# Diagonal and first-level products of the gated recurrence issued in one step

## The chip, the cores and the metric

The kernel runs on one core of one Trainium2 chip. The metric is the device time of one execution in microseconds, as a median of several runs. The engines are TensorE (PE, with its weight loads PEld), VectorE (DVE), ScalarE (ACT), GpSimd (POOL) and SyncE (SP), which issues nearly all DMAs. A matmul writes to PSUM, which has eight banks; the others read from there.

## The reference

One layer of a hybrid decoder for 1024 prompt tokens and 64 sample tokens: a gated feed-forward, then a mixer of sliding-window attention and a gated linear recurrence side by side, then a second gated feed-forward. Only the recurrence is touched by the change. For each of four heads (keys and values 128 wide), with a forget gate f and k = 1 - f, it computes in chunks

```python
def step(S, inp):
    qb, kb, gb, vb = inp                      # gb = log f
    G = jnp.cumsum(gb, axis=2)
    diff = G[:, :, :, None, :] - G[:, :, None, :, :]
    decay = jnp.exp(jnp.where(causal, diff, -jnp.inf))
    A = jnp.einsum('bhtk,bhsk,bhtsk->bhts', qb, kb, decay)
    o = jnp.einsum('bhts,bhsv->bhtv', A, vb) + jnp.einsum('bhtk,bhkv->bhtv', qb * jnp.exp(G), S)
    G_last = G[:, :, -1:, :]
    S = jnp.exp(G_last[:, :, 0, :])[..., None] * S + jnp.einsum(
        'bhsk,bhsv->bhkv', kb * jnp.exp(G_last - G), vb)
    return S, o
```

The entry A[t, s] is the product of q at t and k at s, with every key channel damped by the gates of the positions after s up to t. All is in float32.

## The kernel before

The 1088 tokens are cut into three groups: group 0 has 256 prompt tokens and the 64 sample tokens, groups 1 and 2 have 384 prompt tokens each. Most of the time goes into dense projections; each product of two float32 operands is made of three matmuls over high and low parts (`mm3`, L283 to L285), with the parts formed by a cast on ACT (L260) and a subtraction on DVE or POOL (L261). They write to four PSUM banks with the tag `mm`; everything else shares the other four, tag `ax` (`axbank`).

The recurrence works in blocks of 128 tokens (two in group 0, three in each of groups 1 and 2) and one block of the 64 sample tokens. `intra` (L1256 on) forms the matrix A of a block, transposed, in `At`. It avoids exponentials of sums by a tree: at level h (1, 2, 4 ... 64, for samples up to 4) it pairs neighbouring runs of h tokens, queries from the right run, keys from the left. First Q = q f on DVE (L1264), K = 1 - f on ACT (L1265), `At` is cleared on POOL (L1267), and the products of f over runs of 2, 4, ... tokens are formed on POOL (L1284). The function `blocks` issues one burst of matmuls into one `ax` bank: for four heads, and for each run of 32 tokens, a 32 x 32 product (L1276), 16 matmuls a block, which the trace shows as 32 records. It is called once for the diagonal (`ld`, from K and the unchanged q), whose result DVE multiplies by a 32 x 32 identity into `C` (L1288), and then for each level up to 16 (`lv`, from K and Q), whose result DVE copies into `C` where the level's mask allows (L1295). After each level DVE multiplies the right runs of Q (L1311), and POOL the left runs of K (L1313), by the products of f. Levels 32 and 64 have products of their own (L1300) that ACT copies to `At` (L1303). `hgrn_block` then applies `At` and the carried state to the values, and updates the state; `sample_hgrn` does that for the samples; `finish_hgrn` normalises and gates the output.

All these are Python generators: each `yield` ends a step. The projections of the mixer and the feed-forward products around it call `tick` after each half of a projection (each such call is a unit), and `pace` then lets the two queues of mixer work, attention (`at`) and recurrence (`hg`), take as many steps as they owe:

```python
for k, q in queues.items():
    sofar, rate = 0, 0.0
    for n, _, left in q:
        sofar += left
        rate = max(rate, sofar / max(1, DUE[n] - now[0]))
    owed[k] += rate
```

`left` is the number of steps that a generator still has, given by hand in `ready` (12 for a block, 18 for the sample block), and `DUE` the unit by which group n is to be through (132, 208, 256). Counted in the code, the recurrence of the groups 0, 1 and 2 is handed over at units 36, 128 and 188. What is left over at units 136, 216 and 268 would be run off at once by `need_mix`. A scheduler plans the instructions of each engine from these, by priority and by a simulated time, so that the order on an engine need not be that of the code.

Of the kernel before, what the change touches and what calls it, by code (L numbers as in the profile page):

```python
# [27 lines left out]
NPB = [2, 3, 3]  # L28
# [15 lines left out]
def tile_step(ctx: ExitStack, tc: tile.TileContext, A: dict, O: list):  # L44
# [10 lines left out]
    def uid(s):  # L55
        cnt[0] += 1
        return f"{s}_{cnt[0]}"
# [4 lines left out]
    def axbank(s="ax"):  # L62
        return ps.tile([P, 512], F32, tag="ax", bufs=4, name=uid(s))
# [243 lines left out]
    def new_h(n):  # L307
        return [[hslot(n), hslot(n)], [hslot(n), hslot(n)]]
# [739 lines left out]
    def mixing(tp, h):  # L1048
# [5 lines left out]
        def m2(shape=(P, 512)):  # L1054
            return tp.tile(list(shape), F32, tag="m2", bufs=6, name=uid("m2"))
# [34 lines left out]
        def col_tile(c):  # L1090
# [3 lines left out]
            return load_up(w_in, c * P)  # L1094

        def w_in_units(n, ready):
            w = WIDTH[n]
            npb = NPB[n]
# [157 lines left out]
        def intra(n, c0, r, top, last_q, res):  # L1256

            z = Z[n]
            f, q = [z[i][:, :, c0:c0 + r] for i in ("f", "hq")]
            Q, K, D = m2((P, 4, P)), m2((P, 4, P)), m2()
            V.tensor_tensor(Q[:, :, :r], q, f, op=ALU.mult)  # L1264
            S.activation(K[:, :, :r], f, AF.Copy, bias=1.0, scale=-1.0)  # L1265
            At = tp.tile([P, 4, P], F32, tag="At", bufs=1, name=uid("At"))
            G.memset(At, 0.0)  # L1267
            C = tp.tile([P, 4, 32], F32, tag="cm", bufs=2, name=uid("cm"))
            nq = r // 32

            def blocks(s, x, y):
                b4 = axbank(s).rearrange("p (a t) -> p a t", a=4)
                for a in range(4):
                    for i in range(nq):
                        cs = slice(32 * i, 32 * i + 32)
                        PE.matmul(b4[cs, a, :32], x[:, a, cs], y[:, a, cs], start=True, stop=True)  # L1276
                return b4

            Ds, off, h = [f], 0, 1
            while h <= top:  # L1280
                nx = r // (2 * h)
                Dv = Ds[-1].rearrange("p a (x e) -> p a x e", e=2)
                Ds.append(D[:, off:off + 4 * nx].rearrange("p (a x) -> p a x", a=4))
                G.tensor_tensor(Ds[-1], Dv[:, :, :, 0], Dv[:, :, :, 1], op=ALU.mult)  # L1284
                off += 4 * nx
                h *= 2
            b4 = blocks("ld", K, q)
            V.tensor_tensor(C[:r], b4[:r, :, :32], ident32[:r].unsqueeze(1).to_broadcast([r, 4, 32]),  # L1288
                            op=ALU.mult)
            yield  # L1290
            h = 1
            while h <= top:
                if h <= 16:
                    b4 = blocks("lv", K, Q)
                    V.copy_predicated(C[:r], lmask[h][:r].unsqueeze(1).to_broadcast([r, 4, 32]), b4[:r, :, :32])  # L1295
                else:
                    b4 = axbank(f"l{h}").rearrange("p (a t) -> p a t", a=4)
                    for c in range(0, r, 2 * h):
                        for a in range(4):
                            PE.matmul(b4[c:c + h, a, :h], K[:, a, c:c + h], Q[:, a, c + h:c + 2 * h],  # L1300
                                      start=True, stop=True)
                    for c in range(0, r, 2 * h):
                        S.copy(At[c:c + h, :, c + h:c + 2 * h], b4[c:c + h, :, :h])  # L1303
                if h == min(top, 16):
                    for i in range(nq):
                        G.tensor_copy(At[32 * i:32 * i + 32, :, 32 * i:32 * i + 32], C[32 * i:32 * i + 32])
                nx = r // (2 * h)
                Qv, Kv = [t[:, :, :r].rearrange("p a (x u) -> p a x u", u=2 * h) for t in (Q, K)]
                Dv = Ds.pop(0).rearrange("p a (x e) -> p a x e", e=2)
                if last_q or h < top:  # L1310
                    V.tensor_tensor(Qv[:, :, :, h:], Qv[:, :, :, h:], Dv[:, :, :, 0:1].to_broadcast([P, 4, nx, h]),  # L1311
                                    op=ALU.mult)
                G.tensor_tensor(Kv[:, :, :, :h], Kv[:, :, :, :h], Dv[:, :, :, 1:2].to_broadcast([P, 4, nx, h]),  # L1313
                                op=ALU.mult)
                h *= 2
                yield
            res += [At, Q, K, Ds[0]]

        def finish_hgrn(n, bank, r, c0):
            sm = small()  # L1320
            o = m2((P, 4, P))
            b4 = bank.rearrange("p (a t) -> p a t", a=4)
            for a in range(4):
                S.activation(o[:r, a], b4[:r, a], AF.Square, accum_out=sm[:r, 0, a:a + 1])
            V.tensor_scalar(sm[:r, 0, :4], sm[:r, 0, :4], 1.0 / P, EPS, op0=ALU.mult, op1=ALU.add)
            root(sm[:r, 1, :4], sm[:r, 0, :4])
            V.tensor_tensor(o[:r], b4[:r], sm[:r, 1, :4].unsqueeze(2).to_broadcast([r, 4, P]), op=ALU.mult)
            yield
            tb = axbank("hT").rearrange("p (a t) -> p a t", a=4)
            for a in range(4):  # L1330
                PE.transpose(tb[:, a, :r], o[:r, a], ident[:r, :r])
            m = m2((P, 4, P))
            V.tensor_tensor(m[:, :, :r], tb[:, :, :r], Z[n]["g"][:, :, c0:c0 + r], op=ALU.mult)
            put_mix(n, 1, slice(c0, c0 + r), m[:, :, :r])
            yield

        def hgrn_block(n, b):
            z = Z[n]
            c0 = b * P
            first = state[0] is None  # L1340
            if first:
                state[0] = tp.tile([P, 4, P], F32, tag="st", name="st")
            st = state[0]
            res = []
            yield from intra(n, c0, P, 64, not first, res)
            At, Q, K, D = res
            tb = axbank("kT").rearrange("p (a t) -> p a t", a=4)
            for a in range(4):
                PE.transpose(tb[:, a], K[:, a], ident)
            kn = m2((P, 4, P))  # L1350
            V.tensor_copy(kn, tb)
            yield
            ob = axbank("av")
            for a in range(4):
                PE.matmul(ob[:, a * P:(a + 1) * P], At[:, a], z["v"][:, b, a * P:(a + 1) * P],
                          start=True, stop=first)
                if not first:
                    PE.matmul(ob[:, a * P:(a + 1) * P], Q[:, a], st[:, a], start=False, stop=True)
            yield
            ub = axbank("u").rearrange("p (a t) -> p a t", a=4)  # L1360
            for a in range(4):
                PE.matmul(ub[:, a], kn[:, a], z["v"][:, b, a * P:(a + 1) * P], start=True, stop=True)
            if first:
                V.tensor_copy(st, ub)
            else:
                for a in range(4):
                    V.scalar_tensor_tensor(st[:, a], st[:, a], D[:, a], ub[:, a],
                                           op0=ALU.mult, op1=ALU.add)
            yield from finish_hgrn(n, ob, P, c0)
# [80 lines left out]
        def sample_hgrn():  # L1450
            n, c0, r = 0, 256, NS
            z = Z[n]
            res = []
            yield from intra(n, c0, r, 4, True, res)
            At, Q, K, D = res
            tb = axbank("skT").rearrange("p (a t) -> p a t", a=4)
# [51 lines left out]
        def ready(kind, n):  # L1508
            if n not in MT:
                MT[n] = new_h(n)  # L1510
            if kind == "at":
                gens = [(attn_block(n, b), 9) for b in range(NPB[n])]
                if n == 0:
                    gens += [(sample_attn(), 17), (kv_out(0), 1)]
                if n == 2:
                    gens.append((kv_out(2), 1))
            else:
                gens = [(hgrn_block(n, b), 12) for b in range(NPB[n])]
                if n == 0:
                    gens.append((sample_hgrn(), 18))  # L1520
                if n == 2:
                    gens.append((state_out(), 1))
            queues[kind] += [[n, g, left] for g, left in gens]

        def state_out():
            nc.sync.dma_start(O[4][0, 0].rearrange("h k v -> k h v"), state[0])
            yield
# [55 lines left out]
    h = {}  # L1583
# [195 lines left out]
```

## Time and profile before

| what | us |
|---|---|
| median of three runs | 1987.83 |
| lowest and highest of them | 1987.05, 1988.56 |
| the profiled execution, its own time | 1987.58 |
| its span | 1985.9 |
| mean granted TensorE clock | 0.998 |
| first diagonal product starts | 721.2 |
| last diagonal product starts | 1264.3 |

The profile is of one execution. Its span goes from the first instruction to the last; the time of the execution is 1.7 us longer. The lines of the profile that matter are shown with the prediction, each with what it says.

### The profile page before, as it was taken

What the parts mean: (1) busy time and instruction counts of PE and PEld (TensorE: products, weight loads), DVE (VectorE), ACT (ScalarE), POOL (GpSimd) and SP (SyncE); (2) the same over time, 40 slices, a digit from 0 to 9 for tenths busy, and PEclk for the clock granted to TensorE, in tenths of its full rate; (3) what the DMA queues carried; (4) which work ended last, traced back from release to release, by engine and by line L of the source; (5) the groups of instructions that cost most, each with busy time, mean ns of one, the idle gap of its engine ahead of it and who ended that gap; (6) DMA issues with size and microseconds to landing.
All of it is one profiled execution on the core that took longest, in us unless ns stands there. A gap on an engine that the chain in (4) does not pass through costs nothing.

```text
span 1985.9 us, 34410 instructions
## 1 busy us (share of the span) xinstructions
PE 1969.5 (99%) x13309; PEld 1849.6 (93%) x13309; DVE 1363.3 (69%) x2008; ACT 942.2 (47%) x1672; POOL 593.0 (30%) x559
## 2 busy tenths in 40 slices
PE   9999999999999999999999999999999999999998
PEld 8999999999998987798899898999999999999887
DVE  5876656886557656875566665755988888655666
ACT  6643333444445445644444555655544444444453
POOL 0014323655113101321223423301166565510202
PEclk9999999999999999999999999999999999999999
DMA  8554344656677645765444343556466555577874
GB/s 251 161 154 142 132 173 157 205 185 221 224 242 217 182 134 164 221 194 153 123 107 146 97 124 104 166 161 203 153 196 210 194 194 182 211 232 236 287 261 142
DMA packets 372988, 359.53 MB, mean 181 GB/s; under 512 B 41598, under 2 KB 295369, under 8 KB 372809
## 3 DMA queue, kind: packets, MB, share of 16 engines
q1 hardware_dynamic: 370969, 355.37, 56.8%
q8 instruction: 104, 1.70, 0.4%
q10 hardware_dynamic: 1856, 1.97, 0.3%
q14 instruction: 59, 0.48, 0.1%
HBM read 279.33 MB, written 78.94 MB: 180 GB/s over the span
## 4 chain that ended last, share of the span: by engine, by line
PE 93%; DMA 3%; DVE 2%; ACT 1%; issue 1%; POOL 0%; SPq 0%; DVEq 0%; POOLq 0%; ACTq 0%
PE mm L283 28%; PE mm L285 27%; PE mm L284 27%; PE c L285 1%; PE c L283 1%; PE c L284 1%; PE pv L1240 1%; DMA xt<-in_x_prompt_dram 1%; PE sc L1201 1%; PE lv L1276 1%; PE pT L1227 1%; PE tr L503 1%; DMA ar<-fa 1%; DMA raw<-in_ffn_w_gu_dram 1%; DVE w L261 0%
## 5 line engine op out<-in xcount | busy, mean ns | idle before, releaser
L283 PE MATMUL mm<-h,wsph 128*128 128x320 f32 (+1 forms) x1296 | 416.4, 322 | 0.7 <-ACT wsph L611 0.7
L285 PE MATMUL mm<-h,wspl 128*128 128x320 f32 (+1 forms) x1296 | 410.9, 318 | 1.7 <-DVE wspl L261 1.5
L284 PE MATMUL mm<-h,wsph 128*128 128x320 f32 (+1 forms) x1296 | 410.8, 317 | 0.0
L260 ACT CAST wsph<-raw 128x1024 fp32r<-128x1024 f32 x200 | 209.0, 1047 | 302.2 <-PE mm L284 224.3
L261 DVE TENSOR_TENSOR wspl<-raw,wsph 128x1024 fp32r<-128x1024 f32 x200 | 249.8, 1251 | 143.6 <-ACT wsph L260 142.8
L261 DVE TENSOR_TENSOR w<-raw,w 128x512 fp32r<-128x512 f32 (+1 forms) x226 | 241.6, 1073 | 79.5 <-ACT w L260 77.8
L260 ACT CAST w<-raw 128x512 fp32r<-128x512 f32 (+1 forms) x226 | 169.5, 754 | 244.1 <-PE mm L284 113.8
L283 PEld LDWEIGHTS mm<-h,wsph 128*128 128x128 f32 x1296 | 244.0, 188 | 6.1 <-issue 3.0
L285 PEld LDWEIGHTS mm<-h,wspl 128*128 128x128 f32 x1296 | 243.8, 188 | 3.8 <-DVE wspl L261 1.8
L284 PEld LDWEIGHTS mm<-h,wsph 128*128 128x128 f32 x1296 | 244.2, 188 | 1.9 <-issue 1.4
L283 PE MATMUL mm<-h,w 128*128 128x384 f32 x704 | 235.8, 335 | 0.3 <-DVE big L804 0.3
L284 PE MATMUL mm<-h,w 128*128 128x384 f32 x704 | 235.8, 335 | 0.0
L285 PE MATMUL mm<-h,w 128*128 128x384 f32 x704 | 230.5, 335 | 0.0
L788 POOL TENSOR_TENSOR big<-big 128x384 f32<-128x384 f32 x88 | 113.4, 1288 | 271.4 <-ACT big L801 161.0
L283 PE MATMUL mm<-w,h 128*128 128x512 f32 x462 | 181.8, 396 | 1.8 <-DVE big L984 1.0
L284 PE MATMUL mm<-w,h 128*128 128x512 f32 x462 | 180.5, 391 | 0.0
L285 PE MATMUL mm<-w,h 128*128 128x512 f32 x462 | 179.9, 393 | 0.0
L261 DVE TENSOR_TENSOR w<-t,w 128x512 fp32r<-128x512 f32 x176 | 163.0, 939 | 13.1 <-ACT w L260 13.1
L254 POOL TENSOR_TENSOR sm<-sm,mhalf 128x3 f32<-128x3 f32 (+4 forms) x37 | 35.2, 953 | 394.4 <-DVE sm L338 96.6
L283 PEld LDWEIGHTS mm<-h,w 128*128 128x128 f32 x704 | 132.2, 188 | 0.6 <-DVE big L804 0.6
L284 PEld LDWEIGHTS mm<-h,w 128*128 128x128 f32 x704 | 132.2, 188 | 0.0
L285 PEld LDWEIGHTS mm<-h,w 128*128 128x128 f32 x704 | 131.7, 188 | 0.0
(358 smaller groups left out, 4034.0 us busy)
## 6 DMA issues: line engine op xcount, KB each, us to landing
raw<-in_ffn_w_gu_dram SPq DMA_DIRECT2D x154, 512.0 KB
raw<-in_ffn_w_down_dram SPq DMA_DIRECT2D x74, 512.0 KB
raw<-in_w_in_dram SPq DMA_DIRECT2D x54, 512.0 KB
ar<-fa SPq DMA_DIRECT2D x70, 384.0 KB
big<-in_ffn_w_down_dram SPq DMA_DIRECT2D x88, 256.0 KB
fb<-big SPq DMA_DIRECT2D x44, 512.0 KB
raw<-fb SPq DMA_DIRECT2D x40, 512.0 KB
fa<-big SPq DMA_DIRECT2D x22, 768.0 KB
```

Source lines behind the costliest of these rows:

```text
L254: G.tensor_tensor(y, x, mhalf[:y.shape[0], :y.shape[1]], op=ALU.pow)
L260: S.copy(hi, src)
L261: (lo_eng or V).tensor_tensor(lo, src, hi.bitcast(F32), op=ALU.subtract)
L283: PE.matmul(out, a[0], b[0], start=first, stop=False, skip_group_check=resume)
L284: PE.matmul(out, a[0], b[1], start=False, stop=False, skip_group_check=resume)
L285: return PE.matmul(out, a[1], b[0], start=False, stop=last, skip_group_check=resume)
L503: PE.transpose(bank[:, i * P:(i + 1) * P], y[kh][:, i, k * P:(k + 1) * P], ident)
L788: G.tensor_tensor(e[:, i], e[:, i], e[:, i + 1], op=ALU.mult)
L1201: PE.matmul(banks[g][:, i * 256:i * 256 + wk], zq[64 * g:64 * g + 64, 2 * pr + i, b * P:(b + 1) * P], kx[64 * g:64 * g + 64, k0:k0 + wk], ...
L1227: PE.transpose(bank[:, (i * nk + kb) * P:(i * nk + kb + 1) * P], pt[g][:, i, kb * P:(kb + 1) * P], ident)
L1240: PE.matmul(ob[:, c:c + 64], pT[g][:, (i * nk + kb) * P:(i * nk + kb + 1) * P], vn[:, vb, g * 64:g * 64 + 64], start=kb == 0, stop=kb == n ...
L1276: PE.matmul(b4[cs, a, :32], x[:, a, cs], y[:, a, cs], start=True, stop=True)
```

## The change

The diagonal product and the product of level 1 are issued one after the other, ahead of the masking of the diagonal, and the `yield` between the two is gone. Level 1 then takes the bank that was already filled. The number of steps given to the pacing falls from 12 to 11 for a block and from 18 to 17 for the sample block.

```diff
@@ -1285,13 +1285,13 @@
                 off += 4 * nx
                 h *= 2
             b4 = blocks("ld", K, q)
+            b1 = blocks("lv", K, Q)
             V.tensor_tensor(C[:r], b4[:r, :, :32], ident32[:r].unsqueeze(1).to_broadcast([r, 4, 32]),
                             op=ALU.mult)
-            yield
             h = 1
             while h <= top:
                 if h <= 16:
-                    b4 = blocks("lv", K, Q)
+                    b4 = b1 if h == 1 else blocks("lv", K, Q)
                     V.copy_predicated(C[:r], lmask[h][:r].unsqueeze(1).to_broadcast([r, 4, 32]), b4[:r, :, :32])
                 else:
                     b4 = axbank(f"l{h}").rearrange("p (a t) -> p a t", a=4)
@@ -1515,9 +1515,9 @@
                 if n == 2:
                     gens.append((kv_out(2), 1))
             else:
-                gens = [(hgrn_block(n, b), 12) for b in range(NPB[n])]
+                gens = [(hgrn_block(n, b), 11) for b in range(NPB[n])]
                 if n == 0:
-                    gens.append((sample_hgrn(), 18))
+                    gens.append((sample_hgrn(), 17))
                 if n == 2:
                     gens.append((state_out(), 1))
             queues[kind] += [[n, g, left] for g, left in gens]
```

## The prediction

> **What bounds the kernel now.** I read the page first, for the engine that sets the end, then the chain that ended last, then the stretches of 50 us in which that engine is not full, then the instructions around the products that the change moves.
>
> ```profile
> span 1985.9 us, 34410 instructions
> PE 1969.5 (99%) x13309; PEld 1849.6 (93%) x13309; DVE 1363.3 (69%) x2008; ACT 942.2 (47%) x1672; POOL 593.0 (30%) x559
> ...
> PE 93%; DMA 3%; DVE 2%; ACT 1%; issue 1%; POOL 0%; SPq 0%; DVEq 0%; POOLq 0%; ACTq 0%
> ```
>
> TensorE (PE) is busy for 1969.5 of 1985.9 us, and 93% of the chain lies on it. So an edit can gain in two ways only: by making PE's own work denser, or by closing one of the few gaps, 16.4 us in all. The stretches show where the gaps are (columns: PE busy with its instructions, PEld, DVE, ACT, POOL, granted clock, DMA share, GB/s):
>
> ```profile
> 750.00:800.00 50.00, 48.99 (x323) 39.11 (x322) 35.14 (x66) 29.57 (x62) 10.48 (x18) 1.00 0.53 163
> 800.00:850.00 50.00, 47.92 (x388) 39.63 (x387) 38.90 (x62) 27.83 (x59) 16.11 (x17) 1.00 0.73 220
> ...
> 1100.00:1150.00 50.00, 50.00 (x501) 45.59 (x500) 32.44 (x64) 24.43 (x41) 17.54 (x24) 1.00 0.37 110
> ```
>
> The recurrence runs from the first diagonal product at 721 us to about 1300 us. In that time only the first two of these stretches lose much, 1.01 and 2.08 us, together 3.1 us; DVE is at 70 and 78% there. The third stands for the later blocks: PE without a gap, DVE at 65%. The other gaps lie before, after, or in the tail, where the change has no instruction.
>
> **The change, part by part.** In each of nine blocks (eight of the prompt, one of the samples) the diagonal product `ld`, the first-level product `lv`, and the masking of `ld` move into one step; one `yield` goes. No instruction is added or removed, and no DMA is issued in the steps that move, so SP's queue is passed by nothing but what the shifted pacing brings. What can change is where the product bursts stand on PE, when DVE reads them, and how the steps are spread.
>
> *The bursts.* First an `ld` that stands alone in a stream of projections, then one with `lv` right behind it (start, duration, engine, line, operation):
>
> ```profile
> 963.87 0.34 PE L284 MATMUL mm<-h,wsph 128*128 128x384 f32 x1
> 964.04 0.34 PE L285 MATMUL mm<-h,wspl 128*128 128x384 f32 x1
> 964.31 0.46 PE L1276 MATMUL ld<-big,m 128*32 128x32 f32 x32
> 964.70 0.44 PE L283 MATMUL mm<-h,wsph 128*128 128x384 f32 x1
> 964.98 0.34 PE L284 MATMUL mm<-h,wsph 128*128 128x384 f32 x1
> ```
>
> ```profile
> 1110.56 0.34 PE L284 MATMUL mm<-h,wsph 128*128 128x384 f32 x1
> 1110.83 0.46 PE L1276 MATMUL ld<-big,m 128*32 128x32 f32 x32
> 1111.10 0.49 PE L1276 MATMUL lv<-m,m 128*32 128x32 f32 x32
> 1111.52 0.44 PE L285 MATMUL mm<-h,wspl 128*128 128x384 f32 x1
> 1111.80 0.34 PE L283 MATMUL mm<-h,wsph 128*128 128x384 f32 x1
> ```
>
> In the stream one projection starts 0.17 us after another (963.87 to 964.04). From the last one before the lone burst to the second one behind it takes 964.98 - 964.04 = 0.94 us, where two intervals would be 0.34: a lone burst costs 0.60 us. The same stretch around the pair is 1111.80 - 1110.56 = 1.24 us: the second burst adds 0.30 us. So each pair that stands apart now and together later saves 0.60 - 0.30 = **0.30 us**.
>
> The saving is there because going in and out of a burst costs time: `ld` is 0.39 us from the next start when a projection follows, 0.27 us when `lv` follows. Whether a burst of another shape beside it saves as much is seen where output transposes stand between the two, and where they stand alone:
>
> ```profile
> 1162.14 0.46 PE L1276 MATMUL ld<-big,m 128*32 128x32 f32 x32
> 1162.53 0.66 PE L1180 MATMUL oT<-ident,t 128*128 128x128 f32 x4
> 1163.12 0.46 PE L1276 MATMUL lv<-m,m 128*32 128x32 f32 x32
> 1163.51 0.41 PE L285 MATMUL mm<-h,wspl 128*128 128x320 f32 x1
> ```
>
> ```profile
> 1215.42 0.60 PE L1180 MATMUL oT<-ident,t 128*128 128x128 f32 x4
> 1215.78 0.48 PE L283 MATMUL mm<-wsph,h 128*128 128x512 f32 x1
> ```
>
> `ld` to the transposes is 0.39 us, as to a projection, and the transposes take 0.59 us to the next start with `lv` behind them against 0.36 us with a projection behind. Only the same shape saves. Ordered `ld`, `lv`, transposes, this place takes 0.27 + 0.42 + 0.36 = 1.05 us instead of 0.39 + 0.59 + 0.39 = 1.37, again some 0.3 us. The Trainium skill, TensorEngine Tiling (Array Packing), section Key Properties, says that a change of the tiling mode drains TensorE; the trace agrees, with 0.39 us out of the burst against 0.27 us within it. By that rule alone, a neighbour of another shape would save nothing, which is also what these rows say.
>
> *How many pairs stand apart.* The windows open at each `ld`, 0.6 us long, PE records of L1276 only (the sample block has 16 a burst, the others 32):
>
> ```profile
> 721.20:721.80 0.60, 0.46 (x32) 1.00 0.00 0
> 788.60:789.20 0.60, 0.46 (x32) 1.00 1.12 360
> 867.00:867.60 0.60, 0.45 (x16) 1.00 1.13 342
> 964.30:964.90 0.60, 0.46 (x32) 1.00 0.06 17
> 1035.70:1036.30 0.60, 0.46 (x32) 1.00 0.64 167
> 1110.80:1111.40 0.60, 0.57 (x64) 1.00 1.15 347
> 1162.10:1162.70 0.60, 0.46 (x32) 1.00 0.43 89
> 1210.40:1211.00 0.60, 0.50 (x58) 1.00 0.07 27
> 1264.00:1264.60 0.60, 0.54 (x62) 1.00 0.00 0
> ```
>
> Three blocks already hold about 64 records: the scheduler has put `lv` right behind `ld`, although half a projection lies between them in the code. Nothing is to be had there. Five prompt blocks show 32: 5 x 0.30 = 1.5 us. The sample block has half the records; nothing (if it stays apart) and 0.30 us bound it, I take 0.2. Sum: **-1.7 us**. The bounds of this term are 0, if no pair moves, and 9 x 0.30 = 2.7 us, if all nine counted.
>
> *DVE.* The masking and the predicated copy now become ready together. What they wait for today, and how long a bank is held, shows the block with the fullest DVE:
>
> ```profile
> 782.90 0.68 DVE L1264 TENSOR_TENSOR m<-big,big 128x512 f32<-128x512 f32 x1
> ...
> 793.18 0.28 DVE L1288 TENSOR_TENSOR cm<-ld,ident 128x128 f32<-128x128 f32 x1
> ...
> 798.08 0.29 DVE L1295 COPY_PREDICATED cm<-lm,lv 128x128 f32<-128x128 uint8 x1
> 798.27 0.44 DVE L1311 TENSOR_TENSOR m<-m,big 128x256 f32<-128x256 f32 x1
> ```
>
> Q (L1264) is ready 5 us before its `ld` at 788.6, so `lv` behind `ld` has its operand; the cover is that Q and K are formed when their buffers come free, not in the step. If that cover were gone, `lv` would wait for 0.68 us of DVE. `ld` is read only 4.5 us after it was issued. With both products issued together two of the four `ax` banks are held over that lag. That costs nothing while PE needs no third and fourth bank in it, and up to the DVE work brought forward, 0.29 (L1295) + 0.44 (L1311) = 0.73 us a block, if PE waits for what DVE does next. Bounds: 0 and 9 x 0.73 = 6.6 us. Below nothing I see no reason here, since DVE does the same work. I take 0, as PE does not wait in the block that holds both banks now, at 1111 us: the stretch from 1100 to 1150 us has no gap.
>
> *The pacing.* A group's steps are spread evenly from the unit in which they are handed over to the unit in which they are due. The first group has 2 x 12 + 18 = 42 steps in units 36 to 132, then 2 x 11 + 17 = 39: one step in 2.46 units instead of 2.29. A block's share of the way is 12/42 = 0.286 before and 11/39 = 0.282 after; in the second group it is a third both times. So blocks begin and end where they did, by a unit or two, and the last step is still due at 132, 208 and 256; what follows (output transposes, the projection behind them) is not moved. Inside a block there is more time between levels. What it could free is one row, in which PE waits 1.25 us for a level's operand:
>
> ```profile
> 824.93 0.56 PE L1300 MATMUL l<-m,m 128*32 128x32 f32 x16 [1.25 <-DVE m L1311]
> ```
>
> It is the only such wait, and it lies in the gaps counted above. Which steps fall beside attention steps changes too; as only bursts of one shape save by standing together, I give that nothing, with half a microsecond to either side as an estimate (two pairs of 0.30).
>
> **Sum.** -1.7 us (bursts) + 0 (DVE) + 0 (pacing) = -1.7 us, 0.09%. Against the profiled execution's own span that is 1985.9 - 1.7 = 1984.2 us; its own time was 1987.58 us, 0.25 below the median 1987.83 of the runs shown, so the span and the median differ by a fixed amount and the median goes to **1986.1 us**. A measurement of this kernel can tell about 0.2% from no change, 4.0 us: faster means below 1983.9, slower above 1991.8.
>
> **Rivals.**
>
> 1. *The change doesn't do what it says:* the order on PE is the scheduler's, not the code's. For it: it moved `lv` over half a projection in three blocks. Against it: with nothing between the two in the code and both operands ready 5 us early, it has no ready work of earlier rank to put between. Time: 1987.8. A page bears on a near relative: bursts bound by issue, so that nothing is saved by joining them. Rows speak against that, 0.30 us for the second burst instead of 0.60. The Trainium skill, TensorEngine Tiling (Array Packing), section Instruction Overhead, gives each matmul about 60 cycles whatever its size; the trace does not show that as the limit here. Both together 0.15.
>
> 2. *More is gained:* the wider spacing also closes the gaps of the stretch from 750 to 850 us, 3.1 us. For it: DVE is fullest there and the one wait for a level lies there. Against it: most of that loss has other causes, as the chain's 3% of DMA says, and the change takes no DVE or DMA work away. Time: 1987.8 - 1.7 - 3.1 = 1983.0. Chance 0.10.
>
> 3. *Slower, DVE before evictions:* the joined masking, predicated copy and Q product stand on DVE ahead of the additions that free projection banks, and PE waits. Price 0.73 us a block; 9 x 0.73 - 1.7 = +4.9, time 1992.7. It decides from (4.0 + 1.7)/9 = 0.63 us of wait per block on. For it: the lag of 4.5 us at 788 us. Against it: only two of the 50 us stretches are short of PE work, so two or three blocks pay rather than nine, and those only 1.5 to 2.2 us. Chance 0.13 for slower by over 0.2%.
>
> 4. *A reshuffle in the gapped stretch* without a net direction: the order of evictions, weight splits and loads is planned anew, and the 3.1 us there become up to 6: -1.7 + 3.1 = +1.4, time 1989.2. Chance 0.17.
>
> **How the numbers follow.** The forecast, 1984.8 to 1987.3, has 0.45; with rivals 1 (0.15) and 4 (0.17) that is no measurable change, 0.77, of which I move 0.03 to the two sides. Faster 0.12, same 0.74, slower 0.14. The range goes from a little under rival 2 to just under rival 3: 1982.5 to 1991.5, leaving some 2 in 10 out.
>
> **What would show it.** Right: the nine windows at `ld` all hold about 64 records (32 for the sample block), a stretch of 1.24 us around each, as many instructions as before, PE's gaps outside the tail still about 3 us between 750 and 850 us. Wrong in the first term: records other than L1276 between `ld` and `lv`. Wrong in the DVE term: a wait of PE for L1288 or L1295, or longer waits of L283 for L984, in the list of waits. Wrong in the pacing: PE gaps in the stretch from 1100 to 1150 us, where there are none now. The prediction fails as a whole if the time moves by over 4 us with all pairs joined; then the cause is the order of other work, not the bursts.

## The result: 14 us slower, lost at two places

| kernel | median, us | lowest to highest | profiled span |
|---|---|---|---|
| before | 1988.03 | 1985.99 to 1988.56 | 1985.9 |
| after | 2001.99 | 2000.71 to 2004.07 | 1999.0 |

The ratio is 1.0077, with a 95% interval from 1.0067 to 1.0086. The first lines of the page of the changed kernel:

```profile
span 1999.0 us, 34396 instructions
PE 1974.6 (99%) x13309; PEld 1852.2 (93%) x13309; DVE 1361.2 (68%) x2008; ACT 943.3 (47%) x1672; POOL 594.0 (30%) x559
```

The page hardly changes: PE is busy 99% again, and its 13309 instructions are the same. Of the 13.1 us between the two spans, 8.0 are idle time of PE (1999.0 - 1974.6 = 24.4 against 16.4) and 5.1 are PE being busy for longer (1974.6 against 1969.5). Where the idle time lies is seen in stretches of 50 us of the changed kernel (columns as in the prediction):

```profile
750.00:800.00 50.00, 49.23 (x355) 39.82 (x354) 35.69 (x68) 28.80 (x62) 8.15 (x14) 1.00 0.52 161
800.00:850.00 50.00, 45.40 (x339) 37.44 (x338) 36.88 (x58) 27.60 (x58) 16.22 (x17) 0.93 0.70 210
850.00:900.00 50.00, 47.87 (x367) 41.91 (x367) 36.59 (x81) 22.25 (x48) 12.63 (x14) 0.97 0.66 191
...
1100.00:1150.00 50.00, 50.00 (x484) 44.42 (x483) 35.05 (x70) 24.92 (x48) 20.88 (x27) 1.00 0.32 95
1250.00:1300.00 50.00, 49.12 (x529) 45.69 (x529) 35.34 (x76) 32.59 (x68) 15.51 (x24) 1.00 0.54 171
1300.00:1350.00 50.00, 46.88 (x311) 43.32 (x311) 27.55 (x48) 24.12 (x47) 4.83 (x4) 1.00 0.50 139
```

The same stretches of the kernel before, as far as the prediction does not show them:

```profile
850.00:900.00 50.00, 49.93 (x402) 45.91 (x402) 37.17 (x83) 23.23 (x51) 13.40 (x14) 1.00 0.68 203
1250.00:1300.00 50.00, 50.00 (x556) 47.42 (x555) 37.51 (x80) 34.42 (x73) 13.22 (x22) 1.00 0.48 145
1300.00:1350.00 50.00, 50.00 (x296) 45.83 (x296) 24.86 (x32) 23.27 (x42) 5.51 (x5) 1.00 0.57 157
```

Two places lose. From 800 to 900 us PE now idles 4.60 + 2.13 = 6.73 us instead of 2.08 + 0.07 = 2.15; from 1250 to 1350 us 0.88 + 3.12 = 4.00 instead of nothing. The stretch from 1100 to 1150 us, which the prediction had named as the one to watch for the pacing, is as full as before.

The delay can be dated with instructions that both kernels have in the same number and order. This is the timeline of the kernel before: the last eviction of its line on DVE behind the first place, then the first of three evictions on ACT behind the second (start, duration, engine, line, operation).

```profile
1133.90 0.60 DVE L1107 TENSOR_SCALAR big<-mm,cols 128x384 f32<-128x384 f32 x1
...
1339.58 0.59 ACT L1562 COPY big<-mm 128x512 f32<-128x512 f32 x1 [0.54 <-PE mm L285]
```

The same two in the changed kernel:

```profile
1140.01 0.62 DVE L1107 TENSOR_SCALAR big<-mm,cols 128x384 f32<-128x384 f32 x1 [2.51 <-PE mm L285]
...
1351.87 0.59 ACT L1562 COPY big<-mm 128x512 f32<-128x512 f32 x1 [0.53 <-PE mm L285]
```

So 6.1 us are gone by the first and 12.3 by the second; the two places make up nearly all of the 13.1.

What happens at the first place stands in the timeline of PE. Behind 820 us the projections that are ready run out, and the next ones need operands that are transposed first (L460) and then cast (L260). Before:

```profile
823.29 0.39 PE L285 MATMUL mm<-w,h 128*128 128x512 f32 x1
...
825.42 1.20 PE L460 MATMUL tr<-ident,big 128*128 128x128 f32 x9
827.45 0.50 PE L283 MATMUL mm<-w,h 128*128 128x512 f32 x1 [0.82 <-ACT h L260]
...
832.55 0.68 PE L1300 MATMUL l<-m,m 128*64 128x64 f32 x8
```

After:

```profile
821.45 0.40 PE L285 MATMUL mm<-w,h 128*128 128x512 f32 x1
821.78 0.59 PE L1300 MATMUL l<-m,m 128*32 128x32 f32 x16
822.30 1.20 PE L460 MATMUL tr<-ident,big 128*128 128x128 f32 x9
824.87 0.55 PE L460 MATMUL tr<-ident,big 128*128 128x128 f32 x3 [1.36 <-ACT At L1303]
828.58 1.11 PE L1300 MATMUL l<-m,m 128*64 128x64 f32 x8 [3.16 <-POOL m L1313]
829.62 1.54 PE L460 MATMUL tr<-ident,big 128*128 128x128 f32 x6
...
831.67 0.78 PE L283 MATMUL mm<-w,h 128*128 128x512 f32 x1
```

Before, 4.16 us go by from one projection to the next (823.29 to 827.45), and the product of level 64 (L1300, 128x64) comes 5 us later among projections. After, 10.22 us go by (821.45 to 831.67), and the product of level 64 stands inside, ahead of the last transposes, and waits 3.16 us for its keys. POOL was late with those because of what it had in front of them (timeline of POOL, after):

```profile
821.42 1.27 POOL L1000 TENSOR_TENSOR big<-big,big 128x512 f32<-128x512 f32 x1
822.64 3.11 POOL L1306 COPY At<-cm 32x128 f32<-32x128 f32 x4
825.83 2.12 POOL L1000 TENSOR_TENSOR big<-big,big 128x512 f32<-128x512 f32 x1
827.91 0.61 POOL L1313 TENSOR_TENSOR m<-m,m 128x256 f32<-128x256 f32 x1
```

PE also runs slower in and behind such a gap (stretches of the changed kernel, granted clock third from the right; first three of 5 us, then two of half a microsecond at the fall):

```profile
820.00:825.00 5.00, 3.56 (x33) 2.63 (x33) 5.00 (x7) 3.21 (x9) 4.92 (x6) 1.00 0.31 92
825.00:830.00 5.00, 1.84 (x13) 1.48 (x14) 4.36 (x8) 2.83 (x8) 3.56 (x5) 0.61 0.94 290
830.00:835.00 5.00, 5.00 (x24) 4.43 (x23) 3.44 (x7) 3.13 (x7) 0.63 (x1) 0.71 0.49 152
...
825.50:826.00 0.50, 0.00 (x0) 0.00 (x0) 0.50 (x2) 0.50 (x2) 0.42 (x2) 1.00 0.92 267
826.50:827.00 0.50, 0.00 (x0) 0.00 (x0) 0.50 (x2) 0.00 (x0) 0.50 (x1) 0.50 1.16 365
```

In the five microseconds at the head of the gap DVE and POOL are full (5.00 and 4.92), as they are there in the kernel before (5.00 and 5.00): neither has time left to prepare an operand earlier. In the ten from 825 us the clock is 0.61 and 0.71; in the kernel before it is 1.00 in the same ten. The Trainium skill, TensorE: Matmul & The Clock Gate, section Why this matters for your kernels, says that idle gaps of TensorE of more than about 3 us set the clock back. The trace bears this out only in part: the clock does fall in this gap, but already at 826.1 us, 0.7 us into the wait of 3.16 us (825.42 to 828.58), and in `q_after_l64_first` below it falls to 0.50 at 828.0 us behind waits of 1.35 and 2.00 us, none of 3.

And the bursts? The first 0.8 us from `ld` on, PE's records of L1276 alone, after (columns: PE busy with its records, clock, DMA share, GB/s):

```profile
721.00:721.80 0.80, 0.76 (x64) 1.00 0.19 18
787.80:788.60 0.80, 0.46 (x32) 1.00 0.80 287
```

The pairs stand together in all blocks but the one at 788 us. The change did to the bursts nearly all that the prediction said, and the time went elsewhere.

### The profile page after: what moved, and what is told of

Read it like the earlier page. It is cut to its first block, busy times and chain, and to the rows that moved or that the text cites. A ratio compares the mean times of both kernels' runs of the same rounds, so it can differ in the third digit from the quotient of the medians.

```text
span 1999.0 us, 34396 instructions
## 1 busy us (share of the span) xinstructions
PE 1974.6 (99%) x13309; PEld 1852.2 (93%) x13309; DVE 1361.2 (68%) x2008; ACT 943.3 (47%) x1672; POOL 594.0 (30%) x559
## 4 chain that ended last, share of the span: by engine, by line
PE 93%; DMA 2%; DVE 2%; issue 1%; ACT 1%; POOL 1%; DVEq 0%; POOLq 0%; SPq 0%; ACTq 0%
PE mm L283 28%; PE mm L284 27%; PE mm L285 27%; PE c L285 1%; PE c L283 1%; PE c L284 1%; PE pv L1240 1%; DMA raw<-in_ffn_w_gu_dram 1%; PE sc L1201 1%; DMA ar<-fa 1%; PE lv L1276 1%; PE pT L1227 1%; PE tr L503 1%; PE l L1300 0%; PE mm L564 0%
## 5 line engine op out<-in xcount | busy, mean ns | idle before, releaser
L283 PE MATMUL mm<-h,wsph 128*128 128x320 f32 (+1 forms) x1296 | 416.1, 322 | 2.6 <-ACT sg L706 1.8
L260 ACT CAST wsph<-raw 128x1024 fp32r<-128x1024 f32 x200 | 209.3, 1048 | 314.6 <-PE mm L284 240.8
L260 ACT CAST w<-raw 128x512 fp32r<-128x512 f32 (+1 forms) x226 | 169.5, 754 | 248.9 <-PE mm L284 115.0
L283 PEld LDWEIGHTS mm<-h,wsph 128*128 128x128 f32 x1296 | 243.8, 188 | 9.1 <-issue 3.5
L283 PE MATMUL mm<-h,w 128*128 128x384 f32 x704 | 235.6, 335 | 0.8 <-DVE big L804 0.8
L283 PE MATMUL mm<-w,h 128*128 128x512 f32 x462 | 182.1, 397 | 0.1
L283 PEld LDWEIGHTS mm<-h,w 128*128 128x128 f32 x704 | 132.1, 188 | 1.2 <-DVE big L804 1.1
```

The source lines that it names most:

```text
L260: S.copy(hi, src)
L283: PE.matmul(out, a[0], b[0], start=first, stop=False, skip_group_check=resume)
```

## The experiments

All kernels compute what the reference does. Every ratio is to the kernel before, run on the same chip beside it (medians of the five batches: 1987.01, 1987.22, 1987.73, 1987.19 and 1987.51 us), with its 95% interval.

### Which part of the change costs the time

The change has three parts: the joined issue, the missing `yield`, and the new counts. Four kernels part them. `a_join_late` joins the products but keeps the number of steps by an empty one ahead of them; `b_join_early` joins them and keeps the `yield` where it was; both use the old counts.

```diff
 # a_join_late, against the changed kernel
+            yield
             b4 = blocks("ld", K, q)
             b1 = blocks("lv", K, Q)
 # b_join_early, against the changed kernel
                             op=ALU.mult)
+            yield
             h = 1
 # both
-                gens = [(hgrn_block(n, b), 11) ...
+                gens = [(hgrn_block(n, b), 12) ...
-                    gens.append((sample_hgrn(), 17))
+                    gens.append((sample_hgrn(), 18))
```

> The diagonal and first-level products stand together in the step where level 1 stood before, with the empty step kept ahead of them, so each block has 12 steps again and levels 2 and up keep their units. Theory 1 (the missing step shifts every later step against the projections, and the time is lost where the shifted steps meet the turn to the next group): the time is that of the kernel before less the saving of the bursts, 1985 to 1988 us. Theory 2 (the joined products themselves cost it, by two banks held and DVE work brought forward): about that of the changed kernel, 1998 to 2004 us. Theory 3 (any new plan of the order lands anywhere): no pattern over this and the next three runs.

> The products stand together in the step where the diagonal stood, and the step is kept behind the masking; 12 steps, levels 2 and up keep their units. Theory 1: 1985 to 1988 us. Theory 2: 1998 to 2004 us, as both banks are held for longer than in the late variant. Theory 3: anything from 1984 to 2004.

`a_join_late` took 1985.07 us (0.9992 [0.9982, 1.0002]), `b_join_early` 1987.48 us (1.0009 [0.9999, 1.0018]). Joining the products late costs nothing; joined early, the kernel takes 2.4 us more than that, about the time before. Three of the ten executions of `b_join_early` took over 1990 us. One of them, 1993.14 us, is the profiled one; it shows a wait of 3.5 us of L1301 (the level products there) for DVE at 829.7 us, and one of 2.5 us of the joined `lv` for DVE at 791.4 us: even this order is near the edge.

`c_step_only` issues level 1 where it was, behind the masking, but leaves the `yield` out, with the new counts. `d_counts_only` is the kernel before with the new counts.

```diff
 # c_step_only, against the kernel before
-            yield
             h = 1
 # c_step_only and d_counts_only
-                gens = [(hgrn_block(n, b), 12) ...
+                gens = [(hgrn_block(n, b), 11) ...
-                    gens.append((sample_hgrn(), 18))
+                    gens.append((sample_hgrn(), 17))
```

> The step between the diagonal and level 1 is taken away and the counts are 11 and 17, but the level-1 product is issued where it was, behind the masking of the diagonal, as in the kernel before. Theory 1: slow as the changed kernel, 1997 to 2004 us, with waits of PE for POOL and DVE near 820 to 890 us. Theory 2: the time before, 1986 to 1989 us, or half the loss if the order of masking and product hardly matters. Theory 3: anything.

> Only the counts are 11 and 17; the code keeps its 12 and 18 steps, so the pacing goes slower than the work left and the last steps come late. Theory 1: not before's time; a shift by a unit or two in either direction, and 1990 to 2004 us if shifted steps cost generally. Theory 2: 1986 to 1989 us. Theory 3: anything.

`c_step_only` took 2001.86 us (1.0078 [1.0063, 1.0093]), the whole loss; `d_counts_only`, whose steps come later than before, 1990.62 us (1.0015 [1.0006, 1.0024]), a small loss. The stretches of `c_step_only` at the two places repeat those of the changed kernel nearly to the hundredth (from 1300 to 1350 us PE is busy for 46.88 us in both); the first of them:

```profile
800.00:850.00 50.00, 45.42 (x339) 37.46 (x338) 37.03 (x58) 27.34 (x58) 16.29 (x17) 0.93 0.68 210
```

Its pairs stand together on PE too, in all nine blocks (64 records of L1276 from 721.80 to 722.60 us): with the `yield` gone the scheduler joins them, whichever way the code issues them. So on PE this kernel is nearly the changed one, and it does not part the missing step from the joining. That joining by itself does not cost the time is what `a_join_late` shows; the loss comes with the missing step.

### Where it is lost, and whether the places are independent

`f_keep_g0` keeps the old number of steps in group 0 alone, `g_keep_g12` in groups 1 and 2 alone.

```diff
 # f_keep_g0, against the changed kernel (g_keep_g12: n > 0)
+            if n == 0:
+                yield
             b4 = blocks("ld", K, q)
...
+                gens = [(hgrn_block(n, b), 12 if n == 0 else 11) ...
```

> The changed kernel with the step given back (as an empty step ahead of the joined products, counts 12 and 18) in group 0 and the sample block alone; groups 1 and 2 keep 11. If the loss behind 820 us belongs to group 0's own steps, it goes (net 6 to 10 us) and the loss behind 1235 us stays (6 us): 1990 to 1995 us. If the whole loss hangs on group 0, 1985 to 1988; if none of it, 2000 to 2004.

> The other half: group 0 and the sample block with 11 and 17, groups 1 and 2 with the step given back. By the same theory the loss behind 820 us stays and that behind 1235 us goes: 1993 to 1998 us. Rival, a new plan lands anywhere: f and g do not add up to the loss of the changed kernel (f's loss plus g's loss within 4 us of 15 us would be adding up).

`f_keep_g0` took 1991.89 us (1.0027 [1.0018, 1.0036]), `g_keep_g12` 1995.46 us (1.0037 [1.0023, 1.0051]). First two stretches of `f_keep_g0`, then the same of `g_keep_g12`:

```profile
800.00:850.00 50.00, 49.03 (x395) 40.56 (x393) 39.69 (x62) 28.63 (x59) 16.27 (x17) 1.00 0.73 221
1250.00:1300.00 50.00, 47.88 (x510) 44.37 (x511) 36.75 (x71) 34.54 (x72) 14.69 (x22) 0.95 0.53 168
```

```profile
800.00:850.00 50.00, 45.46 (x340) 37.75 (x339) 37.91 (x61) 27.16 (x57) 17.67 (x19) 0.97 0.67 210
1250.00:1300.00 50.00, 50.00 (x551) 47.37 (x550) 39.00 (x81) 32.88 (x71) 15.19 (x25) 1.00 0.53 168
```

Each has one of the two losses. 0.27% and 0.37% add to 0.64% of the 0.77%: two separate places, each decided, in these two kernels, by the steps of its own groups. (The profiled execution of `f_keep_g0` took 1995.8 us, 3.9 more than its median, so its rows show more of a loss than most of its executions had.)

### Is it POOL's queue

The wait of level 64 ends with POOL, behind four copies of `C` into `At` of together 3.11 us (L1306). `h_after_act_copy` gives these copies to ACT in the changed kernel; `i_late_act_copy` does so in `a_join_late`.

```diff
-                        G.tensor_copy(At[32 * i:32 * i + 32, :, 32 * i:32 * i + 32], C[32 * i:32 * i + 32])
+                        S.copy(At[32 * i:32 * i + 32, :, 32 * i:32 * i + 32], C[32 * i:32 * i + 32])
```

> The changed kernel with the four copies of the finished diagonal blocks into the matrix A moved from POOL to ACT. In the changed kernel's trace TensorE waits 3.2 us at 828.6 us for POOL's key product of level 32, which stands on POOL behind four such copies (3.1 us) and a 2.1 us addition. If that queue is the cause of the first loss, the wait shrinks to under 1 us and 3 to 8 us come back: 1994 to 1999 us. If POOL was only the last of several late engines (DVE's query product and the evictions come as late), under 2 us come back: 2000 to 2003 us.

> The late joining with 12 steps, with the same four copies on ACT. There TensorE waits for DVE (2.1 us), not for POOL, at the level products, so little is to be had: 1983 to 1986 us. Slower than 1988 us would say that ACT is as short in that stretch as POOL.

`h_after_act_copy` took 2004.26 us (1.0084 [1.0069, 1.0099]), a little above both of its ranges, and `i_late_act_copy` 1987.14 us (0.9997 [0.9988, 1.0007]), above its own: neither gained by the move. The two waits of PE at the first place in `h_after_act_copy`, and one of ACT ahead of them:

```profile
827.71 0.55 PE L460 MATMUL tr<-ident,big 128*128 128x128 f32 x3 [3.57 <-ACT At L1303]
829.86 1.09 PE L1300 MATMUL l<-m,m 128*64 128x64 f32 x8 [1.61 <-DVE h L465]
...
825.57 0.63 ACT L416 ACTIVATE junk<-big 128x512 bf16<-128x512 f32 x1 [1.48 <-POOL big L1000]
```

PE's wait for POOL's keys is gone and others stand in its place, of 3.57 and 1.61 us, for ACT and DVE; 11.48 us go by without a projection there. ACT had done the moved copies by 823.2 us; what made it late was its own wait of 1.48 us for an addition on POOL (L1000). So the four copies alone were not what held the place up, and the engine that ends a wait was one of several that were late together, POOL still among them.

### Is it the missing step, or only where the steps fall

If the phase is what costs, that is, the units in which the steps fall, then the kernel before must slow down when its blocks are left alone and only the unit by which a group's recurrence is due is moved; and the changed kernel must recover by another due. One term in `pace` does it:

```diff
-                rate = max(rate, sofar / max(1, DUE[n] - now[0]))
+                rate = max(rate, sofar / max(1, DUE[n] + SHIFT[n] * (k == "hg") - now[0]))
 # SHIFT, on the kernel before: j_before_due_m4 (-4, 0, 0), p_before_due_g2_m3 (0, 0, -3)
 # SHIFT, on the changed kernel: k_after_due_m4 (-4, 0, 0), l_after_due_p3 (3, 0, 0),
 #        n_after_due_p3_p3 (3, 0, 3), o_after_due_p3_m3 (3, 0, -3)
```

> The kernel before, with the recurrence of group 0 due at unit 128 instead of 132; its attention and the other groups keep their dues, every block keeps 12 steps, nothing is joined. Theory P (the loss is one of phase: it depends on which units group 0's level steps fall into at the turn to group 1, whatever the number of steps): the time moves by more than 2 us from the kernel before, most likely up, 1990 to 2000. Theory S (it is the missing step itself, as less time to prepare or wider steps): 1985 to 1989 us.

> The changed kernel with the recurrence of group 0 due at unit 128. Theory P: the first loss (7 to 10 us behind 820 us) changes by more than 3 us in this run or the next, that is 1988 to 1998 us in the better one; the second loss, of group 2, stays. Theory S: 1999 to 2004 us in both.

> The changed kernel with the recurrence of group 0 due at unit 135, so that its steps come later by up to three units. Theory P: as for the run with 128, one of the two loses clearly less than the changed kernel. Theory S: 1999 to 2004 us.

> The late joining with 12 steps once more, in more rounds, to bound the term of the bursts: -1.7 us by the prediction's sum, a ratio of 0.9991. A ratio whose interval holds 0.9991 and not 1.0000 would show it; one at 1.0000 or above would say that the joined bursts give nothing that can be told.

| kernel | median, us | ratio |
|---|---|---|
| j_before_due_m4 | 2001.44 | 1.0063 [1.0049, 1.0077] |
| k_after_due_m4 | 2002.15 | 1.0069 [1.0054, 1.0084] |
| l_after_due_p3 | 1994.64 | 1.0033 [1.0023, 1.0043] |
| m_join_late_again, the kernel `a_join_late` | 1984.97 | 0.9984 [0.9975, 0.9993] |

The kernel before, with a due 4 units earlier for one group and nothing else changed, is 0.63% slower, a little more than the range given for it, and PE waits at the same place for the same thing. Its longest wait (engine, product and line <- what it waited for: us in total, times, longest) and its stretch:

```profile
PE l L1300 <- POOL m L1313: 3.7, 1, 3.7
```

```profile
800.00:850.00 50.00, 43.65 (x354) 35.80 (x353) 37.45 (x58) 27.41 (x59) 15.55 (x18) 0.97 0.68 206
```

The changed kernel with a due 3 units later, `l_after_due_p3`, loses only the second part (same two stretches as above):

```profile
800.00:850.00 50.00, 48.98 (x389) 39.10 (x389) 39.10 (x66) 27.75 (x60) 15.07 (x17) 1.00 0.69 211
1250.00:1300.00 50.00, 47.88 (x508) 44.47 (x508) 36.63 (x71) 34.45 (x72) 14.70 (x22) 0.94 0.52 167
```

Due 4 units earlier, the changed kernel (`k_after_due_m4`) is as slow as without: earlier still does not help, later does. And the joined products without the shift are faster than the kernel before, by 0.16%. The next three ask the same of the second place.

> The changed kernel with the recurrence of groups 0 and 2 due three units later (135 and 259). Moving group 0 alone gave back 7 of the 14 us. If the second loss, behind 1235 us, is one of phase too, it changes by more than 3 us in this run or the next, that is below 1992 us in the better one. If the missing step itself costs it, both stay at 1993 to 1999 us.

> The changed kernel with group 0 due at 135 and group 2 at 253. As for the run before: phase says that one of the two is below 1992 us, the missing step says that both stay at 1993 to 1999 us.

> The kernel before with the recurrence of group 2 due at 253 instead of 256, all steps kept. Phase: more than 2 us away from the kernel before, up if its due happens to be a good one, 1990 to 1996 us. The missing step as cause: 1985 to 1989 us.

With group 2 due 3 units later as well, the changed kernel is level with the kernel before: 1988.76 us, 1.0007 [0.9998, 1.0017]. It does not reach the joined kernel with the old steps (0.9984). With group 2 due 3 units earlier it is back at 2001.95 (1.0069 [1.0054, 1.0084]), and the kernel before with that shift takes 1993.50 (1.0032 [1.0019, 1.0045]). The two stretches of `n_after_due_p3_p3` at the second place are as full as those of the kernel before, 50.00 us of 50 in both; the later one:

```profile
1300.00:1350.00 50.00, 50.00 (x300) 45.79 (x299) 24.70 (x34) 24.68 (x47) 6.51 (x6) 1.00 0.56 156
```

### Is it one product or all of them

What was left is whether level 64, which waits in the middle of the gap, makes the loss. `q_after_l64_first` puts one step ahead of that product, in the second block of group 0 alone; `r_after_l64_both` in the last block of group 2 too. The steps before it stay in their units.

```diff
                 else:
+                    if h == 64 and (n, c0) in ((0, P),):      # r: ((0, P), (2, 2 * P))
+                        yield
                     b4 = axbank(f"l{h}").rearrange("p (a t) -> p a t", a=4)
```

> The changed kernel with one step put in ahead of level 64 of the second block alone; all steps up to level 32 stay in the units they have in it, level 64 falls two units later (84 instead of 82, counted in the code), the counts stay 11 and 17. Theory, one product standing too early: at the first place the loss comes because level 64 stands on PE ahead of the transposes and projections of the next group and waits for its operand; then the stretch without a projection at 820 us falls from 10.2 to about 3 to 5 us, the first loss goes, and the time is about 1994.5 (as where the whole group was due 3 units later, 1994.6). Rival, the level products in general are too early (level 32 is at 79 instead of 81): the stretch stays at 8 us or more, and the time stays at 1999 to 2003.

> The same, and one step ahead of level 64 of the last block of group 2 too (unit 250 instead of 248). Theory, one product standing too early at both places: about 1988, as where both groups were due 3 units later (1988.8). Rival, at the second place the head of the mixer's end stands wrong as a whole, not this product: the second loss stays, some 6 us, and the time is 1994 to 1996; if neither loss goes, 2000 to 2003.

`q_after_l64_first` took 1997.66 us (1.0052 [1.0037, 1.0067]), between its two theories, but its stretch without a projection stays at 8.49 us, as the rival said. `r_after_l64_both` took 1994.08 (1.0031 [1.0020, 1.0043]). That lies in the range of its rival, but not for the rival's reason: the second place does recover, from 4.00 us of idle time to 0.89, and the first does not. In `q_after_l64_first` level 64 is out of the gap, but another wait has taken part of its place (PE, L1302 is the level product there):

```profile
824.66 0.55 PE L460 MATMUL tr<-ident,big 128*128 128x128 f32 x3 [1.35 <-ACT At L1305]
827.21 1.22 PE L460 MATMUL tr<-ident,big 128*128 128x128 f32 x6 [2.00 <-DVE h L465]
...
829.75 0.79 PE L283 MATMUL mm<-w,h 128*128 128x512 f32 x1 [0.38 <-ACT h L260]
...
835.51 0.68 PE L1302 MATMUL l<-m,m 128*64 128x64 f32 x8
```

The second place in `r_after_l64_both`, where the changed kernel has 46.88:

```profile
1300.00:1350.00 50.00, 50.00 (x320) 46.29 (x320) 25.24 (x47) 26.61 (x52) 5.55 (x5) 1.00 0.52 149
```

The ratio falls by 0.0025 where a later due for the whole group gave 0.0044 (1.0077 to 1.0033), and with both places by 0.0046 of 0.0070 (1.0077 to 1.0007). So moving level 64 alone brings back some half of what a later due brings, with intervals too wide to say it closer. That the levels before it make the rest is likely, since they stay in their early units in these two kernels, but no run moves only them.

The table sets the first place of all kernels side by side. The units are counted in the code; the stretch is the longest time from the start of one projection to that of the next between 812 and 850 us in each trace.

| kernel | level 32 and level 64 of that block fall in unit | no projection for, us |
|---|---|---|
| before | 81, 83 | 4.16 |
| a, i, m (joined, old steps) | 81, 83 | 4.87, 5.06, 3.04 |
| b | 81, 83 | 6.50 |
| d | 83, 85 | 4.38 |
| f; l, n, o; p | 81, 83 | 3.06; 4.22, 4.30, 4.32; 3.04 |
| q, r | 79, 84 | 8.49, 8.25 |
| after, c, h | 79, 82 | 10.22, 10.22, 11.48 |
| g | 79, 82 | 10.11 |
| j | 79, 81 | 9.97 |
| k | 77, 80 | 14.11 |

Level 32 in unit 79 or earlier goes with 8 us and more, in unit 81 or later with 3 to 6.5. At the second place the unit of level 64 in the last block, counted in the same way, sorts the kernels but for one: 248 or earlier in all that idle over 3 us from 1250 to 1350 us (after, c, f, h, k, l, o, p, q), 249 or later in those that idle less than 1 (before, a, b, d, g, i, m, n, r). `j_before_due_m4` has the units of the kernel before in the last block, and still idles 0.88 and 1.21 us in the two stretches there. What decides there beyond the due of group 2 stays open.

## Why the prediction was wrong

**The bursts** (-1.7 us) were right in mechanism, and the price of a pair holds: wherever a prompt block's pair came together in the changed kernel, `lv` starts 0.27 us behind `ld` and the next product 0.42 us behind `lv`, as in the pair that the prediction measured. The sum is borne out less sharply. With the phase kept the joined kernel saved 1.94 us in one batch (1987.01 to 1985.07, with an interval that holds no change) and 2.76 in another (1987.73 to 1984.97; 0.16%, interval 0.07 to 0.25%, which is 1.4 to 5.0 us). In the profiled executions PE's busy time fell from 1969.5 us to 1969.0 and 1967.4, and the second of these has no stretch of lower clock, which costs the kernel before an estimated 1.7 us (see below). So the size fits, to a microsecond or two. The pair that did not join, at 788 us, was not the cover that the prediction had thought of, Q on DVE; the list of waits of the changed kernel has it waiting for another DVE result:

```profile
PE lv L1276 <- DVE sm L1209: 0.8, 1, 0.8
```

This is DVE reading the first attention scores (L1209, through at 789.01 us; `lv` starts at 789.07). The scores lie in the same four `ax` banks, so the joined `lv` may have waited for a bank; no run tests that.

**DVE** (0) was right but for that wait of 0.8 us: no wait of PE for the masking (L1289 in the changed kernel) or L1295 is in the list, nor one of L283 for L984, and `a_join_late`, with the products joined and both banks held, loses nothing. Rival 3, whose price was DVE work brought forward in each block, had no part in the loss.

**The pacing** is the step that failed, the "+ 0 (pacing)" of the sum: "I give that nothing, with half a microsecond to either side". It measured about +16 to +17 us: 14.0 slower, although joining saves 1.9 to 2.8. Its working was correct as far as it went: blocks do begin and end within a unit or two of where they did, and no gap came in the stretch from 1100 to 1150 us. But it looked at the ends of the blocks only. The step taken out stands at the head of a block, so the levels behind it come earlier even though the steps are wider: in the second block level 32 falls in unit 79 instead of 81, level 64 in 82 instead of 83. And the conclusion that a unit or two cost nothing was wrong. At the turn from one group to the next the projections run out for some 4 us; after the change level 64 stands inside that turn instead of behind it, and the transposes that feed the next projections come behind it on PE (828.58 and 829.62 us). The prediction tested the pacing where PE had most in reserve, in a stretch without a gap, and not where it had least, in the row that it had quoted itself (the wait of 1.25 us at 824.93) and hoped to see shortened.

**Rival 4** was right in kind, with the order in the gapped stretch planned anew, and wrong in size, because it took the gaps that were there (3.1 us from 750 to 850) as a measure of what could come. Idle time there became 0.77 + 4.60 = 5.4 us, within its 6, but 2.1 more came from 850 to 900 us and 4.0 from 1250 to 1350, where there had been none. Rival 1 has a true part, as `c_step_only` shows: the order on PE is the scheduler's, and the `yield`, not the order of the product and the masking in the code, had kept the pairs apart.

The last sentence of the prediction held: the time moved by over 4 us with all but one of the pairs joined, and the cause is the order of other work.

**What stays open.** Of the 13.1 us between the spans, 8.0 are idle time. PE's extra 5.1 us of busy time are explained in part by the lower clock. In the changed kernel it is at 0.50 from 826.1 to 833.0 us, with 4.4 us busy, and at a mean of 0.57 from 890.5 to 894.5, with 4.0 busy; in the kernel before once, at 0.57 from 909.5 to 913.5, with 4.0 busy. Busy time times what is missing of the clock gives an estimate of 2.2 + 1.7 us against 1.7, so 2.2 of the 5.1. The rest of it is not assigned. Bursts cut into more pieces at the second place would fit (level 32 of the last block is issued as 2 products at 1298.80 us and 14 at 1299.35, with transposes between, where the kernel before has 16 in one), but no run tests that. At the second place, the 4.00 us of idle time include 1.2 of level 64 waiting for DVE (L1311) and 1.8 of projections waiting for ACT (L706); why these come late there was not followed up.

## What to carry to other kernels

In a program whose side work is spread by a count of steps, removing a step is two edits: the one that is meant, and a shift of all that follows in the group. Price the second at the place where the main engine has least in reserve, a turn where its ready work runs out, and not from how far the blocks move on average; moving the due of one group in the unchanged kernel by three or four units shows in one run how sharp that place is. When an edit is worth having, keep the phase and take the edit: the joined products with an empty step in the place of the one removed (`m_join_late_again`, 0.9984 [0.9975, 0.9993]) beat both kernels here, by 0.16% over the kernel before.

## What the runs showed of the hardware that was not expected

The clock can fall without an idle gap of PE. One stretch of the kernel before shows it, with the timeline of PE around its start:

```profile
910.00:915.00 5.00, 5.00 (x41) 4.35 (x40) 2.57 (x7) 0.94 (x1) 0.00 (x0) 0.70 0.53 145
```

```profile
908.32 1.12 PE L1484 MATMUL su<-t,m 32*128 32x512 f32 x2
909.37 0.52 PE L284 MATMUL mm<-h,wsph 128*128 128x384 f32 x1
909.69 0.52 PE L285 MATMUL mm<-h,wspl 128*128 128x384 f32 x1
```

PE is busy for all of 5.00 us at a granted clock of 0.70, and the projections there start 0.32 us apart (909.37 to 909.69) instead of 0.17. It begins behind matmuls of 32 rows (L1484, operand 32x512). Whether work on so few rows counts as rest for the clock was not tried, and it does not always bring the fall: in the traces of `a_join_late` and `m_join_late_again` the clock is at 1.00 behind the same matmuls. A share of 99% for PE says nothing of how near its next gap is: moving one group's due by 4 units, with all instructions the same, cost 0.63%. And the work that stands ahead of the longest wait need not be what to take away: with 3.11 us of copies moved from POOL to ACT, PE waited 3.57 us for ACT instead, which had itself waited for another instruction of POOL.
